# Three projections of an encoder block as paired half products, split between the mixers and a stage of their own

## The chip, the cores and the metric

The kernel runs on one core of a Trainium2 chip. The metric is the device time of one execution in microseconds (us), lower is better. Engines are named as in the profile: PE (TensorE, matrix multiplication), with PEld for its weight loads, DVE (VectorE), ACT (ScalarE), POOL (GpSimd) and SP (SyncE, which here only issues transfers).

## The reference

One layer of a bidirectional encoder, in float32, for 1024 tokens and a width of 1024:

```python
h = rms_norm(x, norm_mix_g)
g_q, g_k, g_v, g_r, lr_f, lr_b, s_q, s_k, s_v, gate_a, gate_b = split(h @ w_in)
y_gla = gla(g_q, g_k, g_v, g_r, lr_f, lr_b) @ w_o_gla   # ends with o * silu(g_r)
y_swa = swa(s_q, s_k, s_v) @ w_o_swa                    # windowed attention
merged = sigmoid(gate_a) * y_gla + sigmoid(gate_b) * y_swa
x = x + merged @ w_out
gate, up = split(rms_norm(x, norm_ffn_g) @ w_ffn_in)
x = x + (silu(gate) * up) @ w_ffn_out
```

The change concerns `g_r`, `gate_a` and `gate_b`, called r, ga and gb in the kernel: each is a product of the normed 1024 x 1024 input with a 1024 x 1024 weight.

## The kernel before

**Numbers.** Each float32 operand of a product is split into a high part (`wh`, `xh`, by ACT) and a low part (`wl`, `xl`, by DVE), and three matmuls (high-high, high-low, low-high) make one product. Nearly all are 128x128 times 128x512. Tokens are treated in two halves of 512 (s = 0, 1).

**Stages.** (1) Load of x, splitting into `xh[k][s]`, `xl[k][s]` (8 row blocks k), the norm's statistics, and the projections q0 and k0 meanwhile (`qk_mm`). (2) The GLA mixer, 45 slots. (3) The attention (SWA) mixer, 22 slots, each of which works on four or five (head group, block) pairs at different stages: squares and norm, turn of q, scores of four heads, softmax, turn of P, output. (4) Gating and the output projections of both branches, and the residual. (5) FFN in, which is already computed as 7 half products in place of 8 (the Winograd form of Strassen's scheme), and FFN out.

**Dense work in the mixers.** The projections that are left are a list, `dense`, of Python generators, each of which gives one matmul at a time: `proj_t` (token-major: v0, v1, skv, sq0, sq1; 192 matmuls each) and `proj_f` (feature-major: q1 to k3, then r0 to r7, ga0, gb0, ... ga7, gb7; 48 matmuls each). `slot(stages, n)` calls the parts of a mixer slot and spreads n matmuls of this list between them with `fill`. In GLA n is 40 (first 6 slots), 31, or 18 at the end; in attention 60 (first 2), 46, or 28 at the end, and `fill(1 << 30)` takes what is left. `need(key)` takes more from the list where a mixer asks for a projection that isn't there yet.

**Weights of the dense work** come as units of 128x512 (`wunit`, L63 to L70): load into `wr` (4 buffers) from SP's queue, `wh` on ACT (L67), `wl` on DVE (L69), 5 buffers each. Units are prepared two ahead (`next_unit`). `proj_t` takes every unit twice, once per token half, and so loads and splits it twice.

**Order.** PE's instructions run in the order in which the program is written (`manual_schedule`). The order on DVE, ACT and SP is set by a scheduler, once, when the kernel is built; every engine then takes its list strictly in order. PSUM has 4 banks of kind "mm" (dense) and 4 of kind "ch" (mixers); the rotation of the latter ties the scores of one attention block to the copies of the turned P of the block before (`ph` on ACT L667, `pl` on DVE L668).

**In attention** the lines are: squares L547, q turned L614 and split (`sqh` L617, `sql` L618), scores L73 with `kTh`, `kTl`, masked maximum on DVE L632, `nm` L641, exp on ACT L647, scaling on ACT L653, P turned L664, split L667 and L668, output on PE L73 with `vSh`, `vSl`, copy `sob` L678.

**In the FFN** the bank `X` takes T2, is read by DVE for u2, and then takes T3 on top. The list `between` puts whole products of other features between the two:

```python
product(X, wsplit(s2, 512), YX["T2"], 4, True, False)
u2 = ctile("u2")
nc.vector.tensor_tensor(u2, X, p1, op=ALU.add)
for p, g in between:
    p(g)
s3 = comb(F.r11, F.r21, ALU.subtract)
product(X, wsplit(s3, 512), YX["T3"], 4, False, False)
```

Of the kernel before, what the change touches and what calls it, by code (L numbers as in the profile page):

```python
# [14 lines left out]
P = 128  # L15
T = 1024
KT = 8
# [7 lines left out]
WARM = 10  # L25
PAD = 672
# [4 lines left out]
def body(tc, i, out):  # L31
    nc = tc.nc
    with ExitStack() as root:
# [70 lines left out]
        stgs = ExitStack()  # L104
        stg = stgs.enter_context(tc.tile_pool(name="stg", bufs=4))
# [35 lines left out]
        def next_unit():  # L141
            while plan and len(ready) <= AHEAD:
                ready.append(wunit(plan.pop(0)))
            return ready.pop(0)

        def proj_f(name, m):
            plan.extend(i["w_f"][m, u] for u in range(2))
# [17 lines left out]
        def proj_t(name, n):  # L165
            for s in range(2):
                plan.extend(i["w_t"][n, k] for k in range(KT))

            def steps():
                for s in range(2):  # L170
# [16 lines left out]
                    for t in range(4):  # L187
# [7 lines left out]
                        scr[name, ti] = d  # L195
            return steps()
# [82 lines left out]
        with tc.manual_schedule(engines={mybir.EngineType.PE}):  # L279
# [7 lines left out]
            for k in range(KT):  # L287
# [17 lines left out]
            for s in range(2):  # L305
                qk_mm(KT - 1, s)
# [179 lines left out]
        def g_turn(hd, c):  # L486
# [6 lines left out]
            for j in range(2):  # L493
# [4 lines left out]
                  proj_t("sq1", 4)] + [proj_f(f"r{m}", 8 + m) for m in range(8)]  # L498
        for m in range(8):
            dense += [proj_f(f"ga{m}", 16 + m), proj_f(f"gb{m}", 24 + m)]  # L500
# [199 lines left out]
        swas.close()  # L700
        xstack.close()
        stgs.close()


        wq = root.enter_context(tc.tile_pool(name="wq", bufs=1))
        x1ss = ExitStack()
# [30 lines left out]
        bs = ExitStack()  # L737
        bms = ExitStack()
        bm = bms.enter_context(tc.tile_pool(name="bm", bufs=1, side="right"))
        bo = bs.enter_context(tc.tile_pool(name="bo", bufs=1))  # L740
        bt = bs.enter_context(tc.tile_pool(name="bt", bufs=2))

        def btile(tag, dt=F32, bufs=None):
            return bt.tile([P, HT], dt, tag=tag, name=nm(tag), bufs=bufs)
# [12 lines left out]
        oa, ob, mh, ml = {}, {}, {}, {}  # L757

        def split_in(o, name, k):
            h = bo.tile([P, HT], FR, tag=f"{name}h{k}", name=nm(name + "h"))  # L760
            l = bo.tile([P, HT], FR, tag=f"{name}l{k}", name=nm(name + "l"))
            nc.scalar.activation(h, o, AF.Copy)
            nc.vector.tensor_tensor(l, o, h.bitcast(F32), op=ALU.subtract)
            return h, l

        def prep_a(s):
            oa[s] = []
            for k in range(KT):
                o = btile("lo")
                nc.sync.dma_start(out=o, in_=scr["o", k, s])  # L770
                r = btile("lr")
                nc.sync.dma_start(out=r, in_=scr[f"r{k}", s])
                sg = btile("sg", bufs=1)
                nc.scalar.activation(sg, r, AF.Sigmoid)
                nc.vector.tensor_tensor(r, r, sg, op=ALU.mult)
                nc.vector.scalar_tensor_tensor(o, o, og[:, k % 2:k % 2 + 1], r, op0=ALU.mult, op1=ALU.mult)
                oa[s].append(split_in(o, "oa", k))

        def prep_b(s):
            ob[s] = []  # L780
            for k in range(KT):
                o = btile("lo")
                nc.sync.dma_start(out=o, in_=scr["b", k, s])
                ob[s].append(split_in(o, "ob", k))
# [28 lines left out]
        def out_proj(s):  # L813
            a = acc[:, s * HT:(s + 1) * HT]
            for j, m in enumerate((0, 4, 1, 5, 2, 6, 3, 7)):
                xr = fi.tile([P, HT], F32, tag="lx", name=nm("lx"), bufs=2)
# [395 lines left out]
```

## Time and profile before

| | us |
|---|---|
| median of 3 runs (1682.58, 1683.54, 1683.4) | 1683.4 |
| the profiled execution | 1680.64 |
| its span in the profile | 1678.9 |
| PE busy in the span | 1668.9 (99%) |
| DVE busy | 1179.9 (70%) |
| ACT busy | 866.0 (52%) |

In the rows of the profile, a matmul with 512 columns has a duration of about 0.39 us, but the next one starts 0.23 us after it, since they are pipelined. A row of a group ends with the idle time of its engine ahead of these instructions and what ended it. An engine's idle time costs only where the work of the bound engine waits for it.

### The profile page before, as it was taken

Reading aid. Unit: us, or ns where it says so; the run is one execution under the profiler, and the core shown is the slowest. Engines: PE = TensorE matmul, PEld = TensorE weight load, DVE = VectorE, ACT = ScalarE, POOL = GpSimd, SP = SyncE. Lnnn points to the kernel's source line nnn. Section 1 sums busy time; section 2 is a strip of 40 time slices with the busy share of each in tenths; the row PEclk is TensorE's granted clock in tenths of the full one; section 3 lists DMA queues with packets and bytes.
Section 4 is the critical chain, followed back from the end, with each engine's and each line's share of the span. In section 5 each row is a group of like instructions: output and inputs, shape, how many; then the busy total and the mean of one; then the engine's idle time right before and its main releaser. Section 6 shows DMA issues by size and latency. Waiting matters only on the chain.

```text
span 1678.9 us, 23670 instructions
## 1 busy us (share of the span) xinstructions
PE 1668.9 (99%) x7884; PEld 1387.8 (83%) x7884; DVE 1179.9 (70%) x2454; ACT 866.0 (52%) x1941; POOL 0.2 (0%) x4
## 2 busy tenths in 40 slices
PE   8999999999999999999999999999999999999999
PEld 6888888888888888888888888888888888788887
DVE  8666777774488666537673568987778877789755
ACT  7555767775457565545553466533333333344442
POOL 0000000000000000000000000000000000000000
PEclk9999999999999999999999999999999999999999
DMA  6433444444543222238764546343224443596433
GB/s 210 151 110 107 132 130 127 144 138 118 161 151 108 88 95 95 76 105 277 246 221 144 187 126 188 114 141 129 94 88 151 164 150 132 176 325 189 149 96 119
DMA packets 153593, 245.58 MB, mean 146 GB/s; under 512 B 17566, under 2 KB 42910, under 8 KB 153472
## 3 DMA queue, kind: packets, MB, share of 16 engines
q1 hardware_dynamic: 153472, 244.08, 45.1%
q8 instruction: 62, 1.02, 0.3%
q14 instruction: 59, 0.48, 0.1%
HBM read 176.90 MB, written 67.11 MB: 145 GB/s over the span
## 4 chain that ended last, share of the span: by engine, by line
PE 96%; DVE 1%; ACT 1%; issue 1%; DMA 1%; SPq 0%; DVEq 0%; ACTq 0%
PE mm L73 48%; PE ch L73 9%; PE mm L1030 7%; PE mm L885 6%; PE mm L884 6%; PE mm L883 6%; PE ch L1030 5%; PE ch L885 2%; PE ch L884 2%; PE ch L883 2%; PE ch L664 1%; PE ch L490 0%; PE ch L614 0%; PE ch L405 0%; ACT xh L263 0%
## 5 line engine op out<-in xcount | busy, mean ns | idle before, releaser
L67 ACT ACTIVATE wh<-wr 128x512 fp32r<-128x512 f32 x254 | 158.6, 627 | 160.4 <-PE mm L73 146.5
L69 DVE TENSOR_TENSOR wl<-wr,wh 128x512 fp32r<-128x512 f32 x254 | 173.8, 686 | 87.7 <-ACT wh L67 82.4
L73 PE MATMUL mm<-xh,wh 128*128 128x512 f32 x512 | 203.8, 398 | 0.3 <-ACT wh L67 0.3
L73 PE MATMUL mm<-xl,wh 128*128 128x512 f32 x512 | 203.3, 397 | 0.2 <-DVE xl L264 0.2
L73 PE MATMUL mm<-xh,wl 128*128 128x512 f32 x512 | 169.3, 397 | 0.0
L73 PE MATMUL mm<-wh,xl 128*128 128x512 f32 x320 | 126.9, 397 | 0.0
L73 PE MATMUL mm<-wh,xh 128*128 128x512 f32 x320 | 126.6, 396 | 0.0
L73 PE MATMUL mm<-wl,xh 128*128 128x512 f32 x320 | 126.4, 395 | 0.0
L857 ACT ACTIVATE wh<-ws 128x512 fp32r<-128x512 f32 x88 | 55.5, 632 | 114.5 <-PE mm L884 68.3
L73 PEld LDWEIGHTS mm<-xl,wh 128*128 128x128 f32 x512 | 96.4, 188 | 17.5 <-DVE xl L264 0.6
L73 PEld LDWEIGHTS mm<-xh,wh 128*128 128x128 f32 x512 | 96.4, 188 | 17.4 <-issue 0.5
L73 PEld LDWEIGHTS mm<-xh,wl 128*128 128x128 f32 x512 | 95.0, 188 | 17.4 <-DVE wl L69 0.8
L857 ACT ACTIVATE wh<-a 128x512 fp32r<-128x512 f32 x66 | 41.7, 632 | 92.3 <-PE ch L1030 42.3
L857 ACT ACTIVATE wh<-wr 128x512 fp32r<-128x512 f32 x52 | 32.9, 632 | 91.0 <-issue 49.3
L858 DVE TENSOR_TENSOR wl<-a,wh 128x512 fp32r<-128x512 f32 x66 | 45.4, 689 | 40.9 <-ACT wh L857 39.8
L1030 PE MATMUL mm<-hh,wh 128*128 128x512 f32 x176 | 68.6, 390 | 0.9 <-DVE c L968 0.9
L73 PEld LDWEIGHTS mm<-wh,xh 128*128 128x128 f32 x320 | 60.2, 188 | 11.1 <-ACT st L193 0.3
L73 PEld LDWEIGHTS mm<-wl,xh 128*128 128x128 f32 x320 | 60.2, 188 | 10.9
L73 PEld LDWEIGHTS mm<-wh,xl 128*128 128x128 f32 x320 | 60.2, 188 | 10.6
L1030 PE MATMUL mm<-hl,wh 128*128 128x512 f32 x176 | 68.6, 390 | 0.1
L1030 PE MATMUL mm<-hh,wl 128*128 128x512 f32 x176 | 68.5, 389 | 0.0
L647 ACT ACTIVATE p<-p,nm,rs 128x384 f32<-128x384 f32 (+1 forms) x64 | 42.8, 671 | 49.0 <-DVE nm L641 49.0
(513 smaller groups left out, 4416.6 us busy)
## 6 DMA issues: line engine op xcount, KB each, us to landing
wr<-in_w_fi_dram SPq DMA_DIRECT2D x102, 256.0 KB, 2.9
wr<-in_w_t_dram SPq DMA_DIRECT2D x80, 256.0 KB, 2.7
wr<-in_w_f_dram SPq DMA_DIRECT2D x64, 256.0 KB, 2.7
B<-c SPq DMA_DIRECT2D x44, 256.0 KB, 2.1
T<-tx SPq DMA_DIRECT2D x44, 256.0 KB, 2.6
a<-in_w_fo_dram SPq DMA_DIRECT2D x44, 256.0 KB, 5.3
hr<-T SPq DMA_DIRECT2D x44, 256.0 KB, 2.6
hr<-B SPq DMA_DIRECT2D x33, 256.0 KB, 4.6
```

The source lines that it names most:

```text
L67: nc.scalar.activation(h, raw, AF.Copy)
L69: nc.vector.tensor_tensor(l, raw, h.bitcast(F32), op=ALU.subtract)
L73: nc.tensor.matmul(o, a, b, start=start, stop=stop)
L647: nc.scalar.activation(p[:, h, :w], p[:, h, :w], AF.Exp, bias=nm_[:, h:h + 1], scale=a.rs[:, h:h + 1], accum_out=dn[:, h:h + 1])
L664: nc.tensor.transpose(pt[:, h], a.p[:, h, (kb - a.b0) * P:(kb - a.b0 + 1) * P], ident)
L857: nc.scalar.activation(h, src, AF.Copy)
L858: nc.vector.tensor_tensor(l, src, h.bitcast(F32), op=ALU.subtract)
L883: nc.tensor.matmul(o, h[:, c], x[kk][0], start=start and kk == 0, stop=False, skip_group_check=True)
L884: nc.tensor.matmul(o, h[:, c], x[kk][1], start=False, stop=False, skip_group_check=True)
L885: nc.tensor.matmul(o, l[:, c], x[kk][0], start=False, stop=kk == nk - 1, skip_group_check=True)
L1030: nc.tensor.matmul(ys[m], a[:, c], b, start=f0, stop=f1, skip_group_check=True)
```

## The change

**Pairs.** r, ga and gb are 24 tiles of 128 features. Tile m and tile m + 4 become a pair (12 of them), and a pair with its two token halves and its two halves of the inner dimension is a 2x2 block product, which is now made with 7 half products of 12 matmuls each, as in the FFN. `first_halves` makes two of the seven (the ones with the unchanged first token half, 24 matmuls per pair, 288 in all) as the last entry of `dense`; after the first 12 the partial sum is stored as "p1" and the bank accumulates on. `second_halves` makes the other five (60 per pair, 720 in all) in a stage of its own behind attention.

**Operands of the second stage.** `xsums(k)` reloads x into four tiles for each of 4 k, norms them (L797), forms the differences (L799 to L805) and splits T1, 22 and T2 into the space of `xh`, `xl` of the second token half and new tiles; `xsums_late` splits T3 and T4 into the space of the first token half. All four `xsums` are called ahead of the last fill, all four `xsums_late` behind it, and then the 12 pairs. The output gating of the first token half (`prep_a(0, k)`) moves into pairs 4 to 11.

**Filling.** `dense` goes from 2400 matmuls to 1536; the slots get GF = 27 (first 24 slots), 20 and 12 matmuls in GLA, SF = 40 (first 2), 17 and 17 in attention.

**Token-major weights** are split once: in the first token half `wkeep` stores both parts of a unit to DRAM from POOL's queue (80 stores), in the second `wagain` loads them from SP's. POOL goes from 8 to 88 instructions in its list, SP from 1069 to 1172.

**Start.** The last `qk_mm` comes ahead of the norm's statistics on PE and not behind them. Some tiles of single use (`lo`, `lr`, `lx`, `sq`, `tx`) become tiles of the common pool `stage()`.

The diff, cut to what matters:

```diff
+GF = (27, 20, 12)
+SF = (40, 17, 17)
...
+        def wkeep(n, k):
+            h, l = wunit(i["w_t"][n, k])
...
+                nc.gpsimd.dma_start(out=d, in_=v.bitcast(F32))
...
+        def wagain(n, k):
...
+                t = wp.tile([P, 512], FR, tag=tag, name=nm(tag), bufs=5)
+                nc.sync.dma_start(out=t.bitcast(F32), in_=d)
...
+            for f in (wkeep, wagain):
+                plan.extend((lambda f=f, k=k: f(n, k)) for k in range(KT))
...
+                for j in range(0, len(PAIRS), 2):
+                    Y = [mmtile(), mmtile()]
+                    for u in range(2):
+                        for q in range(2):
+                            nme, m = PAIRS[j + q][:2]
+                            h, l = next_unit()
+                            for kk in range(4):
...
+                                    nc.tensor.matmul(Y[q], w[:, c], x, start=f0, stop=f1, skip_group_check=True)
+                                    yield
+                            t = stage()
+                            nc.vector.tensor_tensor(t, Y[q], rstd[:, 0:HT], op=ALU.mult)
...
-                    if k < KT - 1:
-                        qk_mm(k, s)
+                    qk_mm(k, s)
...
-            for s in range(2):
-                qk_mm(KT - 1, s)
...
-                n = 40 if t < 6 else 31 if t < NH * NC + 3 else 18
+                n = GF[0] if t < 24 else GF[1] if t < NH * NC + 3 else GF[2]
...
-                slot([lambda e=e: e[0](*e[1:]) for e in v], 60 if t < 2 else 46 if t < 2 * KT + 2 else 28)
-            fill(1 << 30)
+                slot([lambda e=e: e[0](*e[1:]) for e in v], SF[0] if t < 2 else SF[1] if t < 2 * KT + 2 else SF[2])
...
+        def xsums(k):
+            b = {}
+            for q, kq, s in ((11, k, 0), (12, k, 1), (21, k + 4, 0), (22, k + 4, 1)):
...
+                nc.sync.dma_start(out=b[q], in_=i["xT"][kq, s])
+                nc.vector.scalar_tensor_tensor(b[q], b[q], g1[:, kq:kq + 1], rstd[:, s * HT:(s + 1) * HT],
+                                               op0=ALU.mult, op1=ALU.mult)
...
+        def second_halves(f):
...
+            s2 = comb(s1, r11, ALU.subtract)
+            product(X, wsplit(s2, 512), XT["T2"], 4, True, False)
+            u2 = ntile()
+            nc.vector.tensor_tensor(u2, X, p1, op=ALU.add)
+            s3 = comb(r11, r21, ALU.subtract)
+            product(X, wsplit(s3, 512), XT["T3"], 4, False, False)
...
+            for k in range(4):
+                xsums(k)
+            fill(1 << 30)
+            for k in range(4):
+                xsums_late(k)
+            for f in range(len(PAIRS)):
+                second_halves(f)
+                if f >= 4:
+                    prep_a(0, f - 4)
```

**Where instructions stand now.** First PE in the middle of attention. The rows of before are from one block: scores of the four heads (`ch`, with 128x384 columns) with dense matmuls (`mm`) between them.

```order
L73 MATMUL ch_7961<-kTh,sqh_7846 128x384
L73 MATMUL ch_7961<-kTl,sqh_7846 128x384
L73 MATMUL ch_7961<-kTh,sql_7847 128x384
L73 MATMUL mm_7912<-xh_94,wh_7740 128x512
L73 MATMUL mm_7912<-xl_110,wh_7740 128x512
L73 MATMUL mm_7913<-xh_95,wh_7740 128x512
L73 MATMUL mm_7913<-xl_111,wh_7740 128x512
L73 MATMUL ch_7970<-kTh,sqh_7846 128x384
```

The same place of the changed kernel, from the second head of a block to the turn of the next block's q (L659):

```order
L75 MATMUL ch_7772<-kTh,sqh_7665 128x384
L75 MATMUL ch_7772<-kTl,sqh_7665 128x384
L75 MATMUL ch_7772<-kTh,sql_7666 128x384
L238 MATMUL mm_7756<-xh_92,wh_7552 128x512
L75 MATMUL ch_7778<-kTh,sqh_7665 128x384
L75 MATMUL ch_7778<-kTl,sqh_7665 128x384
L75 MATMUL ch_7778<-kTh,sql_7666 128x384
L238 MATMUL mm_7756<-xl_108,wh_7552 128x512
L238 MATMUL mm_7756<-xh_92,wl_7554 128x512
L659 MATMUL ch_7804<-ident,qn_7596 128x128 x4
```

Between two heads' scores stand one or two dense matmuls, where there were four or five.

Then DVE right behind attention. Before, the last `pl` of attention is followed by evictions of dense banks (L132), weight splits (L69) and the output gating (L775, L776):

```order
L668 TENSOR_TENSOR pl_9147<-ch_9141,ph_9146 128x512
L132 TENSOR_TENSOR st_9179<-mm_9002,rstd 128x512
L132 TENSOR_TENSOR st_9183<-mm_9003,rstd 128x512
L69 TENSOR_TENSOR wl_9262<-wr_9258,wh_9260 128x512
L69 TENSOR_TENSOR wl_9292<-wr_9288,wh_9290 128x512
L775 TENSOR_TENSOR lr_9428<-lr_9428,sg_9430 128x512
```

Now the preparation of the second stage stands there. It begins around st_8395, the partial store of one of the last two pairs (36 dense matmuls come behind the one that it waits for):

```order
L797 SCALAR_TENSOR_TENSOR n_2028_8278<-n_2028_8278,g_70,rstd 128x512
L241 TENSOR_TENSOR st_8395<-mm_8246,rstd 128x512
L797 SCALAR_TENSOR_TENSOR n_2029_8281<-n_2029_8281,g_70,rstd 128x512
L797 SCALAR_TENSOR_TENSOR n_2030_8284<-n_2030_8284,g_70,rstd 128x512
L799 TENSOR_TENSOR n_2028_8278<-n_2028_8278,n_2027_8275 128x512
L797 SCALAR_TENSOR_TENSOR n_2037_8303<-n_2037_8303,g_70,rstd 128x512
L788 TENSOR_TENSOR xl_2034_8293<-n_2030_8284,xh_2033_8292 128x512
```

It ends 55 rows behind st_8395, with the low half of the weights of T2 in the first pair, wl_8520:

```order
L788 TENSOR_TENSOR xl_2085_8474<-n_2049_8337,xh_2084_8473 128x512
L788 TENSOR_TENSOR xl_2087_8478<-n_2057_8359,xh_2086_8477 128x512
L788 TENSOR_TENSOR xl_2089_8482<-n_2059_8365,xh_2088_8481 128x512
L841 TENSOR_TENSOR nt_8515<-ch_8495,nt_8485 128x512
L757 TENSOR_TENSOR wl_8520<-ws_8517,wh_8519 128x512
```

Nothing of all this stood between attention and the dense work behind it before; in the same rows between the two pieces stand the stores st_8417, st_8433 and st_8449 of the last two pairs.

Last, PE in the first pair of the second stage, where the bank mm_8496 is X: the end of T2 (`t2h`, `t2l`) and the start of T3.

```order
L777 MATMUL mm_8496<-t2h_2065_8381,wh_8519 128x512
L778 MATMUL mm_8496<-t2l_2066_8382,wh_8519 128x512
L779 MATMUL mm_8496<-t2h_2065_8381,wl_8520 128x512
L777 MATMUL mm_8496<-xh_2074_8453,wh_8539 128x512
L778 MATMUL mm_8496<-xl_2075_8454,wh_8539 128x512
```

No other matmul stands between them; before, this stage did not exist.

More of the change, by code (lines that the diff above doesn't have):

```diff
@@ new lines, in comb, with product @@
+        def comb(x, y, op):
+            t = wq.tile([P, 512], F32, tag="ws", name=nm("ws"), bufs=4)
+            nc.vector.tensor_tensor(t, x, y, op=op)
+            return t
+        def product(o, w, x, nk, start, stop):
+            h, l = w
+            for kk in range(nk):
+                c = slice(kk * P, (kk + 1) * P)
+                nc.tensor.matmul(o, h[:, c], x[kk][0], start=start and kk == 0, stop=False, skip_group_check=True)
+                nc.tensor.matmul(o, h[:, c], x[kk][1], start=False, stop=False, skip_group_check=True)
+                nc.tensor.matmul(o, l[:, c], x[kk][0], start=False, stop=kk == nk - 1, skip_group_check=True)
@@ new lines, in xsums_late, with ntile, put @@
+        def xsums_late(k):
+            XT["T3"].append(xsplit(xp, f"xh{k}0", f"xl{k}0", raws[k][0]))
+            XT["T4"].append(xsplit(xp, f"xh{k + 4}0", f"xl{k + 4}0", raws[k][1]))
+        nturn = [0]
+        def ntile():
+            q, k = divmod(nturn[0] % 8, 4)
+            nturn[0] += 1
+            tag = f"n{(11, 21)[q]}{k}"
+            return tp.tile([P, HT], F32, tag=tag, name=nm("nt"))
+        def put(key, t):
+            d = scratch("_".join(map(str, key)))
+            nc.sync.dma_start(out=d, in_=t)
+            scr[key] = d
@@ L836, in body @@
         with tc.manual_schedule(engines={mybir.EngineType.PE}):
-            prep_a(0)
             branch_a(0)
             prep_b(0)
-            prep_a(1)
+            for k in range(KT):
+                prep_a(1, k)
             branch_b(0)
```

194 lines of the change are left out of this document (117 added, 77 removed).

## The prediction

> **What bounds the kernel now.** I read the profile page first, then a table by stage, then the places where the change puts something new. The page's busy table and chain:
>
> ```profile
> PE 1668.9 (99%) x7884; PEld 1387.8 (83%) x7884; DVE 1179.9 (70%) x2454; ACT 866.0 (52%) x1941; POOL 0.2 (0%) x4
> PE 96%; DVE 1%; ACT 1%; issue 1%; DMA 1%; SPq 0%; DVEq 0%; ACTq 0%
> ```
>
> TensorE (PE) is the bound nearly everywhere, so a matmul that goes is worth its issue interval, and a matmul that moves is worth nothing, unless the place it leaves then has too little PE work to hide the other engines. The table by stage (PE, weight loads, DVE, ACT, POOL, granted clock) shows how much there is to hide. Its stretches are in order: GLA mixer, first and second half of attention, the dense FFN, and two at the start:
>
> ```profile
> 160.00:360.00 200.00, 200.00 (x1111) 171.06 (x1110) 152.77 (x416) 146.07 (x395) 0.00 (x0) 1.00 0.43 132
> 480.00:600.00 120.00, 120.00 (x608) 101.33 (x607) 89.72 (x291) 79.29 (x258) 0.00 (x0) 1.00 0.34 107
> 600.00:720.00 120.00, 120.00 (x605) 101.26 (x604) 69.09 (x201) 68.25 (x188) 0.00 (x0) 1.00 0.27 88
> 1080.00:1440.00 360.00, 360.00 (x1590) 298.09 (x1589) 285.06 (x461) 124.93 (x208) 0.00 (x0) 1.00 0.40 133
> 26.00:32.00 6.00, 3.26 (x6) 1.25 (x5) 5.77 (x9) 5.17 (x9) 0.00 (x0) 0.77 0.23 50
> 32.00:40.00 8.00, 8.00 (x35) 4.89 (x34) 6.99 (x12) 2.55 (x5) 0.00 (x0) 0.96 0.50 159
> ```
>
> The dense stretch gives the unit of the whole sum: 360 us / 1590 = 0.2264 us per 512-column matmul.
>
> **A, matmuls that go: -32.6.** 24 tiles x 48 = 1152 become 12 pairs x 7 products x 12 = 1008: 144 x 0.2264.
>
> **B, the start: -2.7.** PE's timeline shows one real gap, ahead of the ones-matmuls of the norm:
>
> ```profile
> 28.89 3.50 PE L73 MATMUL ch<-acc,ones 128*128 128x512 f32 x4 [2.74 <-DVE acc L272]
> ```
>
> The last q0/k0 step, 12 matmuls x 0.2264 = 2.7, now stands in that gap and no longer behind it.
>
> **C, the GLA mixer with less filling: +4 (0 to +13).** Of slots there are 20 in the 200 us (one vl split each):
>
> ```profile
> L402 DVE TENSOR_TENSOR vl<-vr,vh 128x256 fp32r<-128x256 f32 x20 | 8.4, 419 | 2.0 <-ACT vh L401 2.0
> L69 DVE TENSOR_TENSOR wl<-wr,wh 128x512 fp32r<-128x512 f32 x48 | 33.0, 689 | 14.6 <-ACT wh L67 14.1 <-issue 0.2
> ```
>
> A slot is 10 us, 31 x 0.2264 = 7.0 of it filling and 3.0 mixer. With 27 it is 9.1, with 20 (11 slots) 7.5. DVE had 152.77/20 = 7.6 per slot, of which 33.0/20 = 1.65 are weight splits; token-major weights are now split once, so about 6.0 + 0.8 = 6.8 remain. The sums still fit under 7.5, the order of hand-offs perhaps not everywhere; the upper end is 1.2 us in each of the 11 slots.
>
> The 80 halves are stored from POOL's queue and reloaded from SP's. No row shows such a store; the nearest is a load that lands in 2.7 us:
>
> ```profile
> wr<-in_w_t_dram SPq DMA_DIRECT2D x80, 256.0 KB, 2.7
> ```
>
> A half's buffer is wanted again some 48 matmuls later (10.9 us), so I price the stores at nothing, to +4 if they are slow; that lies inside C's range. The Trainium skill (SBUF — State Buffer, SBUF: two separate sides) says that a DMA issued from GpSimd's queue can starve for descriptors while VectorE runs certain two-port operations; no run here shows it, and by it only the bound of +4 would be approached.
>
> **D, attention with less filling: +30 (+6 to +54).** Two exp groups, one block apart, and the costs of a block:
>
> ```profile
> 554.88 0.71 ACT L647 ACTIVATE p<-p,nm,rs 128x384 f32<-128x384 f32 x1 [4.46 <-DVE nm L641]
> ...
> 558.36 2.13 ACT L653 ACTIVATE p<-p,rd 128x384 f32<-128x384 f32 x4
> ...
> 564.71 0.34 PE L73 MATMUL ch<-kTh,sqh 128*128 128x384 f32 x1
> ...
> 565.06 0.34 PE L73 MATMUL ch<-kTh,sql 128*128 128x384 f32 x1
> ...
> 570.49 0.60 PE L614 MATMUL ch<-ident,qn 128*128 128x128 f32 x4
> ...
> 570.98 0.71 ACT L647 ACTIVATE p<-p,nm,rs 128x384 f32<-128x384 f32 x1 [2.78 <-DVE nm L641]
> ```
>
> ```profile
> L647 ACT ACTIVATE p<-p,nm,rs 128x384 f32<-128x384 f32 x48 | 33.4, 697 | 43.0 <-DVE nm L641 43.0
> L668 DVE TENSOR_TENSOR pl<-ch,ph 128x512 fp32r<-128x512 f32 x36 | 24.5, 687 | 23.7 <-ACT ph L667 23.3
> L667 ACT ACTIVATE ph<-ch 128x512 fp32r<-128x512 f32 x36 | 20.9, 590 | 1.2 <-PE ch L664 1.2
> L547 ACT ACTIVATE sq<-qr 128x128 f32<-128x128 f32 x48 | 14.4, 306 | 1.8 <-DMA qr<-sq 1.8
> L647 ACT ACTIVATION_READ_ACCUMULATOR p<-p,nm,rs 128x1 f32 x60 | 11.2, 187 | 0.0
> L618 DVE TENSOR_TENSOR sql<-ch,sqh 128x512 fp32r<-128x512 f32 x15 | 10.3, 686 | 1.0
> L547 ACT ACTIVATION_READ_ACCUMULATOR sq<-qr 128x1 f32 x48 | 9.5, 197 | 0.0
> L617 ACT ACTIVATE sqh<-ch 128x512 fp32r<-128x512 f32 x16 | 9.3, 580 | 2.9 <-PE ch L614 2.9
> ```
>
> A slot lasts 570.98 - 554.88 = 16.1 us; with 17 fills in place of 46 PE needs 16.1 - 29 x 0.2264 = 9.5. What the idle times of ACT show (43 us for nm) is the slack that this eats. There is a loop from one block's exps to the next one's, because score banks come free only when the P halves of the block before are copied out. In the early blocks ACT's row has exps, three ph, then the rest: four exps 4 x (0.697 + 0.187) = 3.5, three ph 1.8, pl 0.7, the last head's scores 0.7, two fills 0.45, turn 0.6, sqh 0.58, then on ACT itself a weight split (0.63, taken as long as sqh's kind) and four squares 4 x 0.503 = 2.0; with some ten hand-offs of 0.05, 11.5 us. In the last five blocks the scaling (2.13) stands ahead of two of the ph, and behind sqh come sql and a weight split on DVE, 0.69 each, and three small operations: 3.5 + 0.6 + 2.1 + 1.2 + 0.7 + 0.7 + 0.45 + 0.6 + 0.6 + 1.4 + 0.5 + hand-offs 0.6 = 12.9. So PE waits 2.0 in some eight blocks and 3.4 in five: 16 + 17 = 33, less a little at both ends: 30. Lower bound: ACT's sum alone where key blocks are prepared, 79.29 x 16.1/120 = 10.6 minus about 0.3 for fewer weight splits, against 9.5, in eight blocks, less what a slot can borrow: +6. Upper bound: 3.4 in all 16.
>
> **E, the transition: +27.9 (+24 to +36), and +1.7 of clock.** This is the new stage's price. DVE's order has, behind the first partial store that waits for PE (st_8395, released when 36 fill matmuls are left), 55 operations of 512 columns up to and with wl_8520, the low half that the second product T2 needs: 14 of the kind scalar_tensor_tensor, 41 others. Their nearest rows:
>
> ```profile
> L876 DVE TENSOR_TENSOR ws<-wr,wr 128x512 f32<-128x512 f32 x44 | 30.2, 685 | 8.7 <-DMA wr<-in_w_fi_dram 5.6 <-issue 3.1
> L264 DVE SCALAR_TENSOR_TENSOR xl<-xr,g,xh 128x512 fp32r<-128x512 f32 x16 | 11.3, 743 | 2.5 <-ACT xh L263 2.3
> ```
>
> With the store itself 14 x 0.743 + 42 x 0.685 = 39.2 us. PE has 36 fills, the 12 matmuls of T1 and 2 of T2 to put beside them, 50 x 0.2264 = 11.3. The rest is idle: 27.9. It shows in two pieces, since the last fill unit also waits for a store (st_8417) that DVE reaches 37 operations after st_8395. Nothing runs ahead: the 16 x loads of this stage wait on SP behind the last attention stores, as the memory was the mixer's. If these are late, it is +36.
>
> A gap costs clock as well: the two start-up stretches above, after 2.74 us of idling, had 0.77 of the clock for 6 us and 0.96 for 8, 0.23 x 6 + 0.04 x 8 = 1.7 us. I take one such loss. The Trainium skill (TensorE: Matmul & The Clock Gate, Part 1: The HAM clock gate) puts the fall to half clock after about 3.4 us without work, and about as long to come back; by that each of the two pieces would cost at most some 1.7 us as an estimate, the same size. The trace fell already at 2.74 us.
>
> **F, a bank used twice in a row: +11.3 (+9 to +13).** In each pair T2 and T3 accumulate in the same bank X, and u2 is read out between them (VectorE). In the old FFN, where the same scheme stands, the last matmul and the read look so:
>
> ```profile
> 1245.77 0.39 PE L885 MATMUL mm<-b213h,wl 128*128 128x512 f32 x1
> ...
> 1246.20 0.69 DVE L904 TENSOR_TENSOR g<-mm,rstd 128x512 f32<-128x512 f32 x1 [0.45 <-PE mm L885]
> ```
>
> There other products stand between. Here T3 comes right behind: matmul 0.39, hand-off 0.04, read 0.69, hand-off about 0.05, against an interval of 0.23: 0.94 us x 12 pairs.
>
> **G, the rest of the second stage: 0 (0 to +6).** A pair takes PE 60 x 0.2264 = 13.6 us, DVE 15 to 18 operations x 0.685 = 10.3 to 12.3; the loads (2.7 us) go out a pair ahead. Output gating for the first token half, now between pairs 4 to 11, is in that count; what left the branches behind it was hidden there, so it gains nothing.
>
> **The sum.** -32.6 - 2.7 + 4 + 30 + 27.9 + 1.7 + 11.3 + 0 = +39.6. On the profiled execution, 1680.6 (span 1678.9), that is 1720.2; that run lies 2.8 below the median of the three runs, 1683.4, so I forecast 1723.0.
>
> **The rivals.** (1) PE stays the bound throughout: loops and transition are covered, and only A and B count: 1683.4 - 35.3 = 1648.1; with F alone, 1659.4. For it speaks the 99% of PE and the idle time of all others; against it the fixed order of 56 DVE operations against 50 matmuls. It decides if DVE got past them within about 11 us. The Trainium skill (Perfetto Trace Analysis, Identifying the Most-Contended Engine) would have the busiest engine improved first, and this change does that; on the average of the page it promises rival 1, by stages it doesn't. Chance 0.12. (2) The mixers stay covered, since the loops have more room than I count, but E and F stand: -35.3 + 29.6 + 11.3 = +5.6, 1689.0. For it: ACT and DVE sums in the second half of attention (68.25 and 69.09 of 120) are under 9.5 per slot. Chance 0.20. (3) The longer loop holds in all 16 blocks, and 11 GLA slots stall by 1.2: -35.3 + 54 + 13 + 29.6 + 11.3 = +72.6, 1756.0. Chance 0.20. That the change saves other than 144 matmuls can be excluded from its loops.
>
> **How the numbers follow.** The forecast's case has 0.48. The range goes from 1684, below rival 2 with C and D at nothing and E at its lower end, to 1758, just above rival 3; left out are rival 1 and a worse case than (3) of 0.06. A measurement here can tell about 0.2%, 3.4 us, from no change. Faster: rival 1 and a little of rival 2's lower edge, 0.13; same 0.04; slower 0.83.
>
> **What would show it.** In the changed profile: some 144 fewer matmuls on PE; no gap ahead of the norm's ones-matmuls; in attention, PE idle with releasers on DVE (score banks) or ACT, and exp groups 11 to 13 us apart; between the last attention matmul and the first T2, about 28 us of PE idle in two pieces while DVE is full; and 12 gaps of 0.7 us ahead of T3, released by DVE's u2. It is wrong if PE stays at 99%, or if exp groups come every 9.5 us.

## The result, and the profile after

The changed kernel takes 1740.8 us (median of 4 runs, 1736.37 to 1745.62), against 1682.99 (4 runs, 1682.23 to 1683.54) for the kernel before, in turns on the same chip: a ratio of 1.0351 (95% interval 1.0334 to 1.0369). It is slower by 58 us; the forecast was 40. The profiled execution took 1737.7 (span 1735.9), 57.1 more than that of before, at a mean clock of 0.983 where before had 1.0.

The page's busy table and the chain:

```profile
PE 1664.8 (96%) x7740; PEld 1371.7 (79%) x7740; DVE 1252.4 (72%) x2586; ACT 876.2 (50%) x1957; POOL 43.6 (3%) x84
PE 79%; DVE 9%; ACT 6%; DMA 4%; issue 2%; SPq 1%; ACTq 0%; DVEq 0%
```

There are 144 matmuls fewer (7884 to 7740), yet PE's busy time fell by 4 us and not by 33: what is left runs slower in places. PE's share of the chain fell from 96% to 79%. The waits of PE say what stands there now (line waited at, releaser, us, times, longest):

```profile
PE mm L238 <- ACT xh L787: 19.9, 1, 19.9
PE mm L777 <- DVE nt L845: 18.5, 11, 2.5
PE ch L634 <- issue: 4.3, 1, 4.3
PE mm L75 <- ACT oah L787: 3.1, 1, 3.1
PE ch L75 <- ACT kTh L636: 3.0, 2, 2.9
PE mm L779 <- DVE wl L757: 3.0, 1, 3.0
```

The first and the last are the transition, the second is the wait for u2 in the pairs, the third and fifth are the start of attention, the fourth is the start of the branches. The table by stage (PE, weight loads, DVE, ACT, POOL, granted clock, DMA share, GB/s): the start, GLA, three stretches at the start of attention, its middle, the transition, the pairs, the dense FFN.

```profile
26.00:32.00 6.00, 5.92 (x22) 3.41 (x21) 5.97 (x9) 5.89 (x10) 2.50 (x5) 1.00 0.29 95
160.00:360.00 200.00, 198.32 (x1140) 170.30 (x1139) 146.21 (x426) 146.55 (x421) 19.50 (x36) 1.00 0.63 201
400.00:420.00 20.00, 15.47 (x61) 11.73 (x59) 16.02 (x58) 12.26 (x58) 0.00 (x0) 0.83 0.81 262
420.00:440.00 20.00, 15.71 (x74) 13.25 (x74) 16.71 (x80) 14.28 (x66) 0.00 (x0) 0.83 0.52 181
440.00:460.00 20.00, 18.19 (x89) 15.00 (x88) 17.62 (x69) 17.57 (x55) 0.00 (x0) 0.91 0.26 84
480.00:600.00 120.00, 116.19 (x612) 94.25 (x611) 94.48 (x303) 103.82 (x303) 0.00 (x0) 1.00 0.39 122
620.00:640.00 20.00, 6.75 (x20) 5.42 (x21) 19.54 (x32) 11.99 (x19) 0.00 (x0) 0.55 0.41 141
740.00:830.00 90.00, 78.65 (x321) 62.90 (x320) 55.48 (x86) 23.55 (x39) 0.00 (x0) 0.94 0.43 138
1080.00:1440.00 360.00, 360.00 (x1588) 297.75 (x1587) 291.33 (x469) 141.64 (x235) 0.00 (x0) 1.00 0.40 133
```

The dense FFN is as before, and the gap of the start is gone (PE 5.92 of 6 us, before 3.26). GLA keeps 99% and the middle of attention 97%. What was lost lies in three places: the start of attention (49.4 of 60 us busy, clock 0.83, 0.83 and 0.91), the transition (620 to 640: a third busy, while DVE is full), and the pairs (87% at a clock of 0.94).

An account by stage: its length, less 0.2264 us for each dense matmul in it, in both kernels. The rest is what is not dense work, and its growth is the cost.

| | predicted | measured |
|---|---|---|
| A, matmuls | -32.6 | -32.6 |
| B and C, start and GLA to the first turn of k (L634; L589 before) | +1.3 | +5.8 (122.8 to 128.6) |
| D, from there to attention's last output matmul | +30 | +24.2 (93.3 to 117.5) |
| E, transition to T2, clock included | +29.6 | +27.4 |
| F, the wait for u2, and G in the pairs | +11.3 | +28.2 |
| G, the first matmul of the branches | 0 | +4.3 |
| sum | +39.6 | +57.3 |

It adds up to the 57.1 of the two profiled executions. One line is far off, the pairs. Two timelines of PE behind a wait for u2 there show why; first the second pair, then one in which the gating runs beside it (start, duration, instruction, idle time ahead and its releaser):

```profile
664.28 0.47 PE L777 MATMUL mm<-xh,wh 128*128 128x512 f32 x1 [0.88 <-DVE nt L845]
664.59 0.40 PE L778 MATMUL mm<-xl,wh 128*128 128x512 f32 x1
```

```profile
760.71 0.76 PE L777 MATMUL mm<-xh,wh 128*128 128x512 f32 x1 [2.29 <-DVE nt L845]
761.26 0.63 PE L778 MATMUL mm<-xl,wh 128*128 128x512 f32 x1
...
764.20 0.40 PE L779 MATMUL mm<-xh,wl 128*128 128x512 f32 x1
```

The first gap is the one of term F, and PE goes on at full speed. The second is 2.29, and the matmuls behind it last 0.63 and start 0.43 us apart: eight of them take 764.20 - 760.71 = 3.49 us, where 8 x 0.2264 = 1.81. The clock takes 1.7 us more. It doesn't do so behind each such gap; two stretches of 6 us, around this gap and around the last one (2.39 us, at 812.42):

```profile
760.00:766.00 6.00, 5.29 (x16) 4.33 (x17) 4.31 (x8) 1.26 (x2) 0.00 (x0) 0.72 0.00 0
812.00:818.00 6.00, 5.58 (x25) 4.65 (x26) 3.52 (x6) 1.27 (x3) 0.00 (x0) 1.00 0.12 44
```

There are eleven gaps and not twelve: in the last pair four matmuls of the branches (826.12 to 826.80) stand between T2 and T3, and PE waits for nothing there. Six of the eleven are over 2 us (2.06 to 2.46). Four of them, of 2.26, 2.15, 2.29 and 2.06, have 0.72 in such a stretch, 0.28 x 6 = 1.7 us each; the two longest, 2.46 and 2.39, have 1.00. What DVE and ACT did ahead of that gap:

```profile
758.60 0.63 ACT L869 ACTIVATE sg<-st 128x512 f32<-128x512 f32 x1 [2.42 <-DMA st<-r]
759.27 0.69 DVE L870 TENSOR_TENSOR st<-st,sg 128x512 f32<-128x512 f32 x1 [2.24 <-ACT sg L869]
759.88 0.68 DVE L845 TENSOR_TENSOR nt<-mm,nt 128x512 f32<-128x512 f32 x1
```

DVE's list has a gating operation (L870) ahead of u2 (L845). It waits for ACT's sigmoid, which waits for the load of r. u2, whose data is ready, stands behind a load that has nothing to do with it.

### The profile page after: what moved, and what is told of

It is laid out like the page before. It is cut to its first block, busy times and chain, and to the rows that moved or that the text cites. A ratio compares the mean times of both kernels' runs of the same rounds, so it can differ in the third digit from the quotient of the medians.

```text
span 1735.9 us, 23918 instructions
## 1 busy us (share of the span) xinstructions
PE 1664.8 (96%) x7740; PEld 1371.7 (79%) x7740; DVE 1252.4 (72%) x2586; ACT 876.2 (50%) x1957; POOL 43.6 (3%) x84
## 4 chain that ended last, share of the span: by engine, by line
PE 79%; DVE 9%; ACT 6%; DMA 4%; issue 2%; SPq 1%; ACTq 0%; DVEq 0%
PE mm L75 27%; PE mm L777 7%; PE mm L779 7%; PE mm L778 7%; PE mm L1148 7%; PE ch L75 6%; PE ch L1148 5%; PE ch L777 3%; PE ch L779 3%; PE ch L778 3%; PE mm L238 2%; DMA st<-r 2%; ACT p L692 1%; DMA wr<-in_w_f_dram 1%; DMA kvr<-skv 1%
## 5 line engine op out<-in xcount | busy, mean ns | idle before, releaser
L756 ACT ACTIVATE wh<-ws 128x512 fp32r<-128x512 f32 x136 | 86.0, 633 | 216.0 <-PE mm L778 106.2
L69 ACT ACTIVATE wh<-wr 128x512 fp32r<-128x512 f32 x190 | 119.0, 630 | 109.3 <-PE mm L75 85.3
L71 DVE TENSOR_TENSOR wl<-wr,wh 128x512 fp32r<-128x512 f32 x190 | 130.2, 687 | 43.1 <-ACT wh L69 40.7
L75 PE MATMUL mm<-wh,xh 128*128 128x512 f32 x320 | 128.6, 402 | 0.1
L757 DVE TENSOR_TENSOR wl<-ws,wh 128x512 fp32r<-128x512 f32 x136 | 93.2, 686 | 13.5 <-ACT wh L756 13.4
L756 ACT ACTIVATE wh<-wr 128x512 fp32r<-128x512 f32 x64 | 40.6, 634 | 113.8 <-issue 49.7
L238 PE MATMUL mm<-xh,wh 128*128 128x512 f32 x96 | 40.3, 420 | 19.9 <-ACT xh L787 19.9
L777 PE MATMUL mm<-xh,wh 128*128 128x512 f32 x96 | 40.9, 426 | 18.5 <-DVE nt L845 18.5
L770 DVE TENSOR_TENSOR ws<-wr,wr 128x512 f32<-128x512 f32 x68 | 46.9, 690 | 14.3 <-DMA wr<-in_w_f_dram 6.4
L1121 DVE TENSOR_TENSOR hl<-hr,hh 128x512 fp32r<-128x512 f32 x77 | 52.8, 687 | 5.6 <-ACT hh L1120 5.5
L75 PE MATMUL mm<-oah,wh 128*128 128x512 f32 x128 | 50.5, 395 | 3.1 <-ACT oah L787 3.1
L1120 ACT ACTIVATE hh<-hr 128x512 fp32r<-128x512 f32 x77 | 47.7, 619 | 8.1 <-DMA hr<-B 4.2
```

Source lines behind the costliest of these rows:

```text
L69: nc.scalar.activation(h, raw, AF.Copy)
L71: nc.vector.tensor_tensor(l, raw, h.bitcast(F32), op=ALU.subtract)
L75: nc.tensor.matmul(o, a, b, start=start, stop=stop)
L238: nc.tensor.matmul(Y[q], w[:, c], x, start=f0, stop=f1, skip_group_check=True)
L756: nc.scalar.activation(h, src, AF.Copy)
L757: nc.vector.tensor_tensor(l, src, h.bitcast(F32), op=ALU.subtract)
```

## The experiments

The theory when they began: the sum's terms were right in kind (fixed DVE work in the transition, the u2 wait, thin filling in the mixers), with the loss of clock as the part that was mis-sized. The rival: a wait that the prediction did not see, of the gating or of the stores from POOL's queue, makes up most of the difference. Ratios are against the kernel before, on the same chip.

**1. Only the filling of attention (kernel before).**

```diff
-                slot([...], 60 if t < 2 else 46 if t < 2 * KT + 2 else 28)
+                slot([...], 40 if t < 2 else 17)
```

> The kernel before, with only the attention slots' filling cut to the changed kernel's numbers (40 in the first two, then 17); the dense matmuls that this frees run behind attention instead. PE does the same matmuls. Theory (a loop through ACT and DVE of 11.5 to 13 us per block against 9.5 us of PE): +24 to +30 us, about 1709, with exp groups 11 to 13 us apart and PE idle on score banks. Rival (the other engines stay covered at 17): 1683, PE still at 99%.

Measured: 1694.2 us, ratio 1.0068 (1.0051 to 1.0085), +11 us, clock 0.999. PE's longest waits besides the start:

```profile
PE ch L73 <- ACT kTh L591: 2.4, 1, 2.4
PE ch L73 <- DVE pl L668: 1.8, 4, 0.7
PE ch L73 <- DVE kTl L592: 1.4, 3, 0.7
```

The others are of 1.4 us in all or less: no wait recurs once per block for 2 us. The loop of term D isn't there as argued, and thin filling of attention alone costs 11 us where +24 to +30 was expected.

**2. Only the filling of GLA (kernel before).**

```diff
-                n = 40 if t < 6 else 31 if t < NH * NC + 3 else 18
+                n = 27 if t < 24 else 20 if t < NH * NC + 3 else 12
```

> The kernel before, with only the GLA slots' filling cut to the changed kernel's numbers (27, 20, 12); what this frees runs later. Theory: GLA is nearly covered, +0 to +8 us, so 1683 to 1691. Rival (the mixer's hand-offs bind in the slots with 20): +13 us and more, 1696.

Measured: 1688.84 us, ratio 1.0039 (1.0024 to 1.0054), +5.6 us, inside what was expected for term C.

**3. Another order of the products (changed kernel): 22 between T2 and T3, so that 12 matmuls stand there, and T4 behind T1 of the next pair.**

```diff
+            while later:
+                later.pop(0)()
             s2 = comb(s1, r11, ALU.subtract)
             product(X, wsplit(s2, 512), XT["T2"], 4, True, False)
...
+            product(Z, wsplit(s4, 512), XT["22"], 4, False, True)
...
             product(X, wsplit(s3, 512), XT["T3"], 4, False, False)
...
+            later.append(last)
```

> The changed kernel, with the fourth product of a pair (22) put between T2 and T3, and the last one (T4) behind the next pair's T1, so that no bank is read and used again at once; same matmuls, same bytes. Theory (the second stage loses 28 us over its matmuls by the bank read, which in pairs 4 to 11 is queued behind the gating's wait for a load): PE has 12 matmuls more of cover (2.7 us) for a wait of 0.9 to 2.5 us, so nearly all goes: about -25 us, 1715. Rival (the second stage is bound by DVE's or ACT's work per pair): the waits move to other products, less than -8 us.

Measured: 1710.32 us, ratio 1.0165 (1.015 to 1.0181), 30.5 less than the changed kernel's 1740.8.

```profile
PE mm L238 <- ACT xh L787: 20.8, 1, 20.8
PE mm L777 <- DVE nt L849: 2.9, 3, 1.6
```

The wait for u2 falls from 18.5 to 2.9 and the transition stays. The gain is twice the 15.6 us of waiting: with the gaps, the slow matmuls behind them went too (the clock is 1.00 in all stretches from 650 to 820). By the account the pairs now lose 3.9 us and not 28.2; the rest of the gain lies at the first matmul of the branches (3.9) and ahead of the pairs.

**4. The output gating behind the pairs (changed kernel).**

```diff
                 second_halves(f)
-                if f >= 4:
-                    prep_a(0, f - 4)
+            for k in range(KT):
+                prep_a(0, k)
```

> The changed kernel, with the output gating of the first token half taken out of pairs 4 to 11 and put behind all pairs; the order of products is as it was. Theory (in those pairs the read of u2 on DVE stands behind a gating step that waits for the load of r): waits ahead of T3 fall from about 2.3 to 0.9 us in eight pairs and the clock stays up there, -22 us in the stage; behind it the gating of the first blocks is exposed, some 4 to 8 us, so about 1723. Rival (the long waits come from the bank itself or from DVE's load): the waits stay at about 2 us and the time does not fall.

Measured: 1748.35 us, ratio 1.0394 (1.0378 to 1.0409): 7.5 more, not less. The waits, and a stretch of the pairs and what follows them:

```profile
PE mm L75 <- ACT oah L787: 16.2, 8, 6.8
PE mm L777 <- DVE nt L845: 11.4, 12, 1.8
```

```profile
750.00:800.00 50.00, 46.50 (x202) 37.35 (x201) 29.92 (x46) 10.23 (x17) 0.00 (x0) 1.00 0.38 125
800.00:840.00 40.00, 27.50 (x98) 18.84 (x96) 20.70 (x31) 11.24 (x18) 0.00 (x0) 0.81 0.52 158
```

Half of the expectation held: without gating the pairs wait 11.4 us in all and the clock stays at 1.00; by the account they lose 14.7 us in place of 28.2. The other half failed: the gating is no cheaper behind them. It becomes a chain of load, sigmoid, two multiplications and a split for each of eight blocks, for which the branches' first matmuls wait 16.2 us and then run slowly.

**5. Both fillings (kernel before).** The edits of 1 and 2 together.

> The kernel before with both fillings cut to the changed kernel's numbers, GLA and attention; all dense matmuls that are left over run behind attention. Theory (the two costs measured apart, +11 and +5.6, just add): about 1700, and no long gap where attention begins. Rival (the lower filling at GLA's end is also what makes the 4.25 us gap and the low clock at the start of attention in the changed kernel): 1708 to 1713, with that gap.

Measured: 1712.56 us, ratio 1.017 (1.0155 to 1.0185), +28.6 us. The parts do not add up: 11 and 5.6 make 16.6. Three stretches of its attention stage, which begins at 410.9:

```profile
420.00:440.00 20.00, 17.58 (x92) 13.72 (x91) 19.36 (x87) 17.92 (x75) 0.00 (x0) 1.00 0.32 94
440.00:460.00 20.00, 15.81 (x78) 12.94 (x77) 18.88 (x76) 18.59 (x65) 0.00 (x0) 0.91 0.40 112
460.00:480.00 20.00, 17.56 (x89) 14.50 (x88) 15.65 (x61) 19.65 (x60) 0.00 (x0) 0.91 0.39 125
```

There PE is 85% busy, at a clock that falls to 0.91. The long gap of the rival isn't there (0.8 us ahead of the first turn of k); there are several waits of 1.4 to 2.3 us. By the account's boundaries the start and GLA cost 8.9 us more than before and attention 21.7, close to what they cost in the changed kernel (5.8, with the 2.7 of the start gained, and 24.2). The new theory: it is the start of attention that runs dry, where DVE and ACT are full with turning and splitting keys and queries.

**6. Token-major weights split twice again (changed kernel).**

```diff
-            for f in (wkeep, wagain):
-                plan.extend((lambda f=f, k=k: f(n, k)) for k in range(KT))
+            for s in range(2):
+                plan.extend((lambda k=k: wunit(i["w_t"][n, k])) for k in range(KT))
```

> The changed kernel with the token-major weights loaded and split in both token halves, as before: no stores from GpSimd's queue, 40 more splits each on ACT and DVE. Theory (at the start of attention the transfers are at 96% of their time, by the stores and reloads of halves, so the constants land late): the 4.25 us gap and the clock of 0.83 behind it go, -8 to -12 us, about 1731, if the 40 splits stay hidden. Rival (the gap comes from the lower filling alone): it stays, and the time is 1741 or a few us more.

Measured: 1736.52 us, ratio 1.0307 (1.029 to 1.0324), 4.3 less than the changed kernel. The 4.3 us ahead of the first turn (L634) are down to 1.4, another 1.6 fall on later turns, and other waits stand near that place:

```profile
PE ch L709 <- ACT sob L723: 4.5, 2, 2.3
```

The theory, -8 to -12 us, is not met. The waits at the start of attention (2.27, 2.26, 1.52 and 1.40 us) are now those of run 5, which has no stores either (2.27, 2.25, 1.53 and 1.40). So the stores and reloads change which waits stand there. Whether they cost time stays open: the ratio is lower than the changed kernel's, but the runs overlap (1733.66 to 1738.68 against 1736.37 to 1745.62), and in the profiles attention ends at 597.7 against 598.2 while the span is 1.0 us longer. They are not what made the difference.

**7. No splits of T3 and T4 (changed kernel).** Their products take the operands of T1 and 22.

```diff
-            XT["T3"].append(xsplit(xp, f"xh{k}0", f"xl{k}0", raws[k][0]))
-            XT["T4"].append(xsplit(xp, f"xh{k + 4}0", f"xl{k + 4}0", raws[k][1]))
+            XT["T3"].append(XT["T1"][k])
+            XT["T4"].append(XT["22"][k])
```

> The changed kernel without the splits of T3 and T4 (8 on ACT, 8 on DVE; the products take the operands of T1 and 22 instead, so r, ga and gb come out as other numbers). Theory (between attention and the first T2, DVE's row of operations sets the time, about 0.605 us each): 8 x 0.605 = -4.8 us, 1736, all of it in the gap ahead of the second product's low half and the stretch behind. Rival (the loads of x or PE's own work set it): 0.

Measured: 1737.13 us, ratio 1.0317 (1.03 to 1.0334), 3.7 less. The runs overlap (1734.7 to 1739.96), so the gain is less sure than its size. The wait at T2 (3.0) is gone, and the one ahead of it is 21.9 us in place of 19.9, now with st as its releaser; by the account E falls by about 2 us. T3's and T4's splits are only the second, short piece of the transition.

**8. Six pairs in place of twelve (changed kernel),** the other tiles as whole projections at the end of `dense`, the products ordered as in 3, gating behind the pairs as in 4, more filling: GF = (28, 24, 14), SF = (50, 30, 20).

```diff
-                  for m, r0 in ((m, base + m) for m in range(4))]
+                  for m, r0 in ((m, base + m) for m in range(4))][4:10]
...
+        dense += [proj_f(f"r{m}", 8 + m) for m in range(8)]
+        dense += [proj_f(f"gb{m}", 24 + m) for m in (2, 6, 3, 7)]
```

> A version built from the findings: only ga's four pairs and two of gb's go the new way (72 matmuls saved), the other tiles stay whole projections and fill the mixers (28, 24, 14 in GLA; 50, 30, 20 in attention) and some 200 matmuls behind attention, which cover DVE's preparation; products in the order T1, T2, 22, T3, next T1, T4; gating behind the pairs. Theory: -16.3 - 2.7 + 3 (mixers) + 3 (what is left of the transition) + 5 (gating) = -8, about 1675. Rival (the transition and the gating stay exposed as they were): +27 + 16 - 19 + 3, about 1710.

Measured: 1721.45 us, ratio 1.0224 (1.0209 to 1.0239). A clear miss, with both costs that were thought avoided still there:

```profile
PE mm L75 <- ACT oah L789: 16.6, 8, 6.8
PE ch L779 <- ACT xh L789: 7.4, 2, 4.3
PE ch L779 <- DVE nt L845: 3.6, 1, 3.6
```

The gating was exposed as in 4. Whole projections at the end did not hide the transition either: they read `xh[k][1]` to their end, into whose space T1 and 22 are split.

**9. Only the start (kernel before).** The last `qk_mm` ahead of the statistics.

```diff
-                    if k < KT - 1:
-                        qk_mm(k, s)
+                    qk_mm(k, s)
...
-            for s in range(2):
-                qk_mm(KT - 1, s)
```

> The kernel before with one edit of the change alone: the last products of q and k in the gated linear attention stage are issued ahead of the norm statistics. Theory: the 2.7 us wait on the evicted accumulator goes, nothing new opens, about 1680.4 us against 1683.0 (-2.7 us, outside 0.2% at the edge). Rival: the time was covered, or the gap moves to the next chain, and the time stays at 1683 +-1.

Measured: 1679.81 us (11 runs, 1677.7 to 1682.72) against 1681.02 (15 runs), ratio 0.999 (0.9981 to 0.9999). The wait on `acc` is no longer among PE's. By medians the gain is 1.2 us, and the interval reaches from 3.2 to 0.2; the expected 2.7 lies in it, no change does not, barely. Of the parts that were tried alone it is the one that pays.

**10. Both fillings, with a richer start of attention (kernel before).**

```diff
-                n = 27 if t < 24 else 20 if t < NH * NC + 3 else 12
+                n = 27 if t < 24 else 20 if t < NH * NC + 3 else 18
...
-                slot([...], 40 if t < 2 else 17)
+                slot([...], 60 if t < 2 else 17)
```

> The kernel before with more filler in both mixer stages, as in the run with both (1712.6 us), but its filler is richest at the start of attention (60 matmuls for the first two blocks, then 17, where the run with both had 40 at once) and at the end of the gated linear attention stage (18 where it had 12). Theory that the two together cost more than their sum because the start of attention runs dry and the clock falls there: about 1700 us (-12). Rival, that each block pays for its own missing filler wherever it lies: 1712 us, as before.

Measured: 1702.08 us, ratio 1.0122 (1.0106 to 1.0139), where 5 had 1.017: 8 to 10 us of the 28.6 came back from 100 matmuls put around one place (six more in each of the last ten slots of GLA, 20 more in each of the first two of attention). The stage starts at 430.7 here, 20 us later than in 5, so the stretches that answer to those of 5 are:

```profile
440.00:460.00 20.00, 16.76 (x85) 13.88 (x84) 18.25 (x73) 15.15 (x60) 0.00 (x0) 0.91 0.32 106
460.00:480.00 20.00, 19.85 (x110) 16.54 (x109) 19.59 (x81) 19.55 (x66) 0.00 (x0) 1.00 0.31 91
480.00:500.00 20.00, 20.00 (x111) 16.79 (x111) 19.15 (x70) 19.74 (x67) 0.00 (x0) 1.00 0.31 92
```

PE idles 3.4 us there where it idled 9.0 in 5, and by the account's boundaries attention costs 13.0 us more than before in place of 21.7 (14.5 in run 1). That the start of attention makes the two fillings cost more than their sum is shown for most of the 12 us of excess, by an edit that adds filler only there and in the slots of GLA just ahead of it.

**11. Six pairs, mended (changed kernel).** As 8, with `prep_a(0, f)` inside the six pairs on tiles of its own, and GF = (28, 24, 18), SF = (60, 29, 20). The first half products stand ahead of the whole projections, as they did in 8 already.

```diff
-            o = stage()
+            o = btile("lo", bufs=1)
...
-            r = stage()
+            r = btile("lr")
...
+                prep_a(0, f)
```

> Six of the twelve pairs made the new way, as in the six-pair run (1721.5 us), but with the first half products ahead of the whole projections, the gating inside the six pairs on tiles of its own, and the filler richest at the start of attention. Theory: the gating's 16.6 us of waits and the slow clock behind them go (-25), the start of attention gives back 3 to 5, the transition's wait stays (about 17): 1690 to 1695 us. Rival, that the gating's loads still stand ahead of the u2 chain on VectorE as in the change: about 1715 us.

Measured: 1692.89 us, ratio 1.0066 (1.0048 to 1.0084), 28.6 less than 8. PE's waits and two stretches, the transition and the pairs behind it:

```profile
PE ch L779 <- ACT xh L789: 11.0, 2, 7.9
PE ch L779 <- DVE nt L845: 2.9, 1, 2.9
PE mm L238 <- DVE st L241: 2.9, 2, 2.0
```

```profile
700.00:740.00 40.00, 31.03 (x107) 23.67 (x108) 36.07 (x60) 15.30 (x25) 0.00 (x0) 0.75 0.41 132
740.00:780.00 40.00, 39.41 (x174) 32.36 (x173) 31.99 (x52) 13.02 (x22) 0.00 (x0) 1.00 0.61 200
```

The wait for `oah` is gone from the list and the pairs run at full clock, with gating among them. What is left is the transition: 11.0 + 2.9 us of waits and 0.8 for `xl` (L780), 14.7 in all, and a clock of 0.75 in the 40 us from 700. The waits for st (2.9) lie elsewhere, at 435.7 and 449.4, about the start of attention. Against that six pairs save 72 x 0.2264 = 16.3 us. So this form, too, loses to the kernel before; of all that ran, only 9 is ahead of it. A transition without this wait wasn't tried.

## Why the prediction came out as it did

**The sign and the reason held.** PE's work moved away from where it hid other engines, and the fixed DVE work of a new stage was exposed. The measured 1740.8 lies 17.8 above the forecast, in its range.

**A held:** 144 matmuls fewer.

**B held in kind.** The gap is gone, and run 9 shows the start alone to gain a little, 1.2 us (0.2 to 3.2).

**C was right for the filling (+4 said, +5.6 in run 2).** The stores were priced at nothing, with +4 as their bound; run 6 is 4.3 us lower by its median, but its profile shows no gain, so the runs don't tell whether they cost anything. The transfers themselves (KB each, median us from issue to landing) were quick:

```profile
wh<-wh POOLq DMA_DIRECT2D x40, 256.0 KB, 3.3
```

The Trainium skill's remark on starving queues (SBUF — State Buffer, SBUF: two separate sides) describes nothing that these stores show. For the 4.3 us ahead of L634 the profile names no releaser ("issue"), but its rows show what the turn waits for: the last step of the keys' norm and turn (qn, L612) ends on DVE at 407.89, and L634 starts at 407.99. That chain goes back to the load of `kvr`, which SP issues at 397.81 behind six loads of constants and which takes 3.98 us; from 380 to 400 the transfers are at 96% of their time.

**D's size was near (+30 said, +24.2 measured), but its reason failed.** The prediction had a loop of 11.5 to 12.9 us per block in some thirteen of the sixteen blocks. The exp groups of the changed kernel's ACT, first of four heads each:

```profile
485.82 0.71 ACT L692 ACTIVATE p<-p,nm,rs 128x384 f32<-128x384 f32 x1
495.67 0.73 ACT L692 ACTIVATE p<-p,nm,rs 128x384 f32<-128x384 f32 x1
...
575.85 0.70 ACT L692 ACTIVATE p<-p,nm,rs 128x384 f32<-128x384 f32 x1
```

With those left out there are nine steps in 90.0 us, 10.0 each, half a microsecond over PE's 9.5. A part of the difference is in the exps: the sum took 0.884 us for each, and the four of the first group start 0.70 apart (485.82, 486.52, 487.21, 487.90). PE idles only 3.8 us between 480 and 600. The cost is at the start: 10.6 us idle between 400 and 460 (60 - 49.4, of which L634's 4.3 counts under C), and the clock of 0.83, 0.83 and 0.91, which over 20 us each would be up to 8.6 more. PE's timeline has the largest gap of D there:

```profile
429.27 0.44 PE L75 MATMUL ch<-kTh,sqh 128*128 128x384 f32 x1 [2.85 <-ACT kTh L636]
```

Another 1.12 us, for `kTl`, follows at once. By the account attention costs 14.5 us more in run 1, where it alone is thin, and 21.7 in run 5, where GLA is thin too; run 10 ties this difference to the start. That the sum was near is chance: a loop too long for the middle, and a start that was "a little at both ends" to be taken off.

**E held (+29.6 said, +27.4 measured),** in two pieces as forecast:

```profile
633.25 0.77 PE L238 MATMUL mm<-xh,wh 128*128 128x512 f32 x1 [19.94 <-ACT xh L787]
...
644.56 0.73 PE L779 MATMUL mm<-t2h,wl 128*128 128x512 f32 x1 [2.99 <-DVE wl L757]
```

22.9 us are idle where 27.9 was said. The profile names ACT's `xh` as what ended the first wait, but the store that the fill needs (st, L241) ends on DVE at 633.11, and DVE is busy with hardly a break from 607 to 638. DVE's operations last 0.69 but start 0.605 apart (759.27, 759.88, 760.48 for L870, L845, L871), so 56 of them take 33.9 us and not 39.2; less PE's 11.3 that is 22.6. The clock took some 4 us more, not 1.7: both pieces, not one, are followed by slow matmuls. That the term came out so near is partly luck, since the two misses have opposite signs.

**F was near: 11.3 said, 14.7 measured in run 4,** where nothing else is in the way. Its 12 waits add up to 11.4 us, but a gap costs more than its idle time. In the second pair the last matmul of T2 starts at 663.01 and the 13th behind it at 667.10, 4.09 us, where 13 x 0.2264 = 2.94: the gap of 0.88 costs 1.15.

**G is the term that was mis-sized: 0 (0 to +6) said, about 18 measured,** 28.2 - 14.7 = 13.5 in the pairs and 4.3 at the branches. The step that failed is the sentence that counted the gating into a pair's DVE sum. The sum did fit (55.48 of 90 us busy); the order did not. The gating takes its tiles from the pool that the pair's results use too; SP issues the load of r at 754.11, behind the store of such a result (753.7), and sigmoid and multiplication stand ahead of u2 in DVE's fixed list. Hence the waits for u2 rise from 11.4 to 18.5, +7.1, and the clock adds 1.7 us to four of them, 6.8. Together that is 13.9, against the account's 13.5. Run 4 shows that these waits come from the gating, run 3 that matmuls between T2 and T3 take all but 3.9 us of the pairs' loss away, and run 11, with interleaved pairs, that gating on tiles of its own does no harm. The two remedies were not parted inside run 11.

**The rivals.** The first (PE stays the bound) is out by E alone. Of the second (the mixers stay covered) half is true: the middle of attention is covered, its start isn't. The third had the mixers' loops at their worst, 1756, which is a little nearer to the measured time than the forecast (15 us against 18), and wrong in where the time goes. The four chances add up to 1.00, so the 0.06 that was named for a case worse than the third had no place beside them.

## What to carry to other kernels

Work that fills the gaps of another stage is worth more than its own time: before thinning it, look at that stage's first blocks, where everything has to be prepared at once, and not at a mean block. A new stage is priced by the fixed work that must be done before its first matmul can start, and an engine's busy sum says nothing on an operation that stands, in that engine's list, behind one waiting for a load. Where a bank is read between two products, put other products between, and count PE's gaps together: several small ones close to one another cost the clock here as one of 2 us did.

## What the runs showed of the hardware

**Short gaps can slow TensorE, and then cost nearly twice.** Behind waits for u2 of 0.88 us, and of 1.83 in the third pair of run 4, the next matmuls went at full speed. Of the six between 2.06 and 2.46 us four were followed by some eight matmuls 0.43 us apart, and which four their length doesn't tell. The Trainium skill (TensorE: Matmul & The Clock Gate, Part 1: The HAM clock gate) gives an activity window of about 3.4 us that runs freely. If so, it depends on where in the window a gap falls, which would fit the four of six; that a gap of 2.06 us is enough doesn't follow from an idle window of that length, and no run here shows the window itself. Nor is 2 us a limit below which nothing happens, since gaps seem to add up: in run 2 waits of 0.94 and 0.70 us, the second ending at 70.97, were followed from 72.13 by eight matmuls 0.43 us apart, and at the start of attention of the changed kernel a wait of 1.69 us (until 452.22) was followed by slow ones from 453.59. In run 4 the same wait was followed by none. While the clock is down, smaller gaps do harm too: in run 4 waits of 0.83 to 2.34 us, one after the other, behind one of 6.76, kept matmuls slow from 827 to past 850.

**VectorE's rows overlap.** Operations on 512 columns last 0.69 us in the trace and start 0.605 us apart when they follow one another, so a chain of them by durations comes out 14% too long.
